# Interleaving the bidirectional scans of a Mamba-2 block with the next group's projections, and moving the decay behind the product of state and C

## The chip, the cores and the metric

The kernel runs on one core of a Trainium2 chip. The metric is device time in microseconds of one launch. The core's engines are TensorE (PE in the profile; PEld is its weight load), VectorE (DVE), ScalarE (ACT) and GpSimd (POOL); SyncE (SP) only issues transfers here. ScalarE and GpSimd issue transfers too.

## What is computed

One encoder block over 1040 tokens (16 learned ones and 1024 of the input), width 1024, all in float32:

```python
u = rms_norm(h, w_norm_mix)
proj = u @ w_in                     # 9344 columns: conf_a, conf_g, z, xbc, dt, gates
c = depthwise_conv31(conf_a * sigmoid(conf_g)); c = silu(layer_norm(c))
xbc = silu(depthwise_conv7(xbc))    # xs: 32 heads x 64; B, C: 4 groups x 128
# each direction d, in chunks of 128 tokens; a_cs is the cumulated dt*A inside a chunk, xd = x*dt
y_diag = (C B^T * exp(a_cs[l] - a_cs[s]) masked) @ xd
states = B^T @ (exp(a_cs[-1] - a_cs) * xd)
S = S * exp(a_cs[-1]) + states                 # from chunk to chunk
y_off = exp(a_cs) * (C @ S_before)
y = y_f + y_b + D * xs
y = rms_norm(y * silu(z)); merged = gates * (c @ w_conf_out), gates * (y @ w_ssm_out)
h = h + merged @ w_out
out = rms_norm(h + expert_choice_ffn(rms_norm(h)))   # 16 experts, 130 tokens each
```

## The kernel before

Everything is kept transposed, channels on the 128 partitions and the 1040 tokens along the free axis. A planner orders the instructions of each engine: it goes through the program in the order written, simulates, and issues what is ready by priority; `tc.high_priority(offset=n)` moves what is inside ahead by n. Each engine, and each queue of transfers, then runs its list strictly in order.

**Projections.** w_in is taken in 73 tiles of 128 columns. `Columns` loads the raw tiles on SP's queue (L191) in groups of four, takes a norm for a scale (L192 to L206), and splits each tile into a high and a low half-precision part (L217, L218), one tile ahead. `proj` multiplies in three pieces of some 346 tokens ("thirds" below), each 24 matmuls (L96 to L98) into one of three PSUM buffers (mm).

**Stage b1** holds dt, four conf tiles, all 24 xbc tiles, eight gate tiles and four z tiles. An xbc tile is convolved with 7 taps on VectorE (L436), passes a Silu (L437), and goes to memory channel-major (xbc_d) and, turned on TensorE, token-major (xk_d). A conf tile has 31 taps (L329) that are spread over what follows by `some_taps`.

**Scans.** For each of four groups of eight heads, `group` walks nine chunks in both directions: 18 calls of `half`. A half loads the row of cumulated decays of its eight heads, copied to all partitions (L512), and the token-major x and B (L506, L510). ScalarE forms E = exp(-relu(cs - row)) (L524, L525) and overwrites the row with exp(row) (L527); VectorE multiplies E by the masked product of B and C (L543) and row by C (L528). TensorE adds both terms in py (L550): xw times E, and the state S times row. VectorE adds py to xs, in the first of the two directions together with the D skip (L558, L555). The new state is made from st_ps (L565, L570, L571); GpSimd makes xw (L516). The unmasked direction's product of B and C goes through memory (cb_d) to the half that needs it later.

The scans have a priority of 3000. Behind every pair of halves one of the remaining projections is written (`filler`): four conf, twelve z and eight gate tiles over the four groups. After the groups come the output products of the SSM branch, whose weights `split_w` splits into buffers of the pool wsp (L158, L159), allocated behind the scans, then the norm of the conf branch, the merge, and 16 experts.

Of the kernel before, what the change touches and what calls it, by code (L numbers as in the profile page):

```python
# [13 lines left out]
OP = mybir.AluOpType  # L14
# [31 lines left out]
def tile_block(ctx, tc, x, meta_tokens, w_norm_mix, w_in, w_conf_dw, b_conf_dw, conf_ln_g, conf_ln_b,  # L46
# [10 lines left out]
    xbc_d = dram.tile([24, P, T], F32, name="xbc_d")  # L57
# [4 lines left out]
    xk_d = dram.tile([NTT, P, 20 * P], F32, name="xk_d")  # L62
    cs_d = dram.tile([64, T], F32, name="cs_d")
    cb_d = dram.tile([GR, NTT, P, P], F32, name="cb_d")
# [71 lines left out]
    wraw = wstack.enter_context(tpool("wraw", bufs=3))  # L136
    mps_stack = ctx.enter_context(ExitStack())
# [24 lines left out]
    with tpool("upool", side="right") as upool, tpool("stage", bufs=2, side="right") as stage, \  # L162
            tpool("bc") as bc, tpool("cfp") as cfp, ExitStack() as ostack:
# [10 lines left out]
        class Columns:  # L174

            def __init__(self, order):
                self.order, self.raw, self.split, self.at, self.groups = order, {}, {}, 0, 0

            def group(self):
                b = 4 * self.groups
                cols = self.order[b:b + 4]
# [4 lines left out]
                sq = w16.tile([P, 4], F32, name="sq")  # L188
                for i, col in enumerate(cols):
                    t = r16.tile([P, KD, P], F32, name="wr16")  # L190
                    nc.sync.dma_start(t, w_in[0][:, col:col + P].rearrange("(k p) c -> p k c", p=P))  # L191
                    act.activation(out=junk, in_=t, func=AF.Square, accum_out=sq[:, i:i + 1])  # L192
                    self.raw[b + i] = t
                sqb = w16.tile([P, 4], BF, name="sqb")
                dve.tensor_copy(sqb[:, :n], sq[:, :n])
                ps = mps.tile([P, 512], F32, name="mm")
                pe.matmul(ps[:, :n], onesb, sqb[:, :n], start=True, stop=True)
                sc = w16.tile([P, 4, 4], F32, name="sc", bufs=3)
                sci = sc.bitcast(I32)
                dve.tensor_scalar_max(sc[:, 0, :n], ps[:, :n], 1e-36)  # L200
                dve.tensor_scalar(sci[:, 0, :n], sci[:, 0, :n], 24, 23, op0=OP.logical_shift_right,
                                  op1=OP.logical_shift_left)
                dve.tensor_scalar(sci[:, 1, :n], sci[:, 0, :n], -1.0, float(204 << 23), op0=OP.mult, op1=OP.add)
                dve.tensor_scalar(sci[:, 2, :n], sci[:, 0, :n], float(50 << 23), None, op0=OP.add)
                dve.tensor_scalar_mul(sc[:, 2, :n], sc[:, 2, :n], su[:, 1:2])
                dve.tensor_scalar_mul(sc[:, 3, :n], sc[:, 2, :n], 0.5)  # L206
# [3 lines left out]
            def convert(self, n):  # L210
# [3 lines left out]
                wh = w16.tile([P, KD, P], F16, name="wh", bufs=3)  # L214
                wl = w16.tile([P, KD, P], F16, name="wl", bufs=3)
                with tc.high_priority(offset=400):
# [4 lines left out]
            def take(self, col):  # L221
# [4 lines left out]
                if n == 0:  # L226
                    self.group()
                    self.convert(0)
                if n % 4 == 0:
                    self.group()  # L230
# [4 lines left out]
        order = [OFF_DT]  # L235
        for i in range(4):
            order += [i * P, D + i * P]
            for m, j in enumerate((4 * i, 4 * i + 1, 4 * i + 2, 4 * i + 3, 16 + i, 20 + i)):
                order.append(OFF_XBC + j * P)
                if m in (2, 5):  # L240
                    order.append(OFF_GATE + (2 * i + (m == 5)) * P)
            order.append(OFF_Z + i * P)
        for g in range(GR):
            order += [(4 + g) * P, D + (4 + g) * P]
            order += [OFF_Z + j * P for j in range(4 + 4 * g, min(8 + 4 * g, 16))]
            order += [OFF_GATE + j * P for j in range(8 + 2 * g, 10 + 2 * g)]
# [1026 lines left out]
```

## Time and profile before

| | us |
|---|---|
| three runs | 3096.0, 3101.21, 3108.91 (median 3101.21) |
| the profiled execution, its own time | 3112.4 |
| its span in the trace | 3110.7 |
| first norm and setup | 0 to 60 |
| projections of stage b1 | 60 to 560 |
| scans with the other projections | 560 to 1262 |
| output products, merge, w_out, routing | 1262 to 1760 |
| experts and final norm | 1760 to 3110 |

Over the span TensorE is busy 90%, VectorE 72%, ScalarE 54%, GpSimd 24%. In the profile's rows, "x" is a count of instructions, "busy" the time in which at least one of a group runs (matmuls are pipelined and overlap, so the mean of one can exceed busy over count), and "idle before" the engine's idle time ahead of them with what ended it. The granted clock is the share of TensorE's full speed that it got.

### The profile page before, as it was taken

What the parts mean: (1) busy time and instruction counts of PE and PEld (TensorE: products, weight loads), DVE (VectorE), ACT (ScalarE), POOL (GpSimd) and SP (SyncE); (2) the same over time, 40 slices, a digit from 0 to 9 for tenths busy, and PEclk for the clock granted to TensorE, in tenths of its full rate; (3) what the DMA queues carried; (4) which work ended last, traced back from release to release, by engine and by line L of the source; (5) the groups of instructions that cost most, each with busy time, mean ns of one, the idle gap of its engine ahead of it and who ended that gap; (6) DMA issues with size and microseconds to landing.
All of it is one profiled execution on the core that took longest, in us unless ns stands there. A gap on an engine that the chain in (4) does not pass through costs nothing. (4 is left out here: it accounts for less than half of the span.)

```text
span 3110.7 us, 65955 instructions
## 1 busy us (share of the span) xinstructions
PE 2787.0 (90%) x28098; PEld 2372.4 (76%) x28098; DVE 2231.9 (72%) x2849; ACT 1684.7 (54%) x2502; POOL 735.0 (24%) x677
## 2 busy tenths in 40 slices
PE   5999999887878788399999798999999999999996
PEld 4666666554545455388987698999999999999996
DVE  5969779486877795867745587767777766677773
ACT  6545445554746464243413376666666666666653
POOL 1101011344544643312000001212222222221213
PEclk9999999997988898699999899999999999999998
DMA  5334233776777665421533598999999999999994
GB/s 158 93 110 137 90 117 126 176 145 190 146 207 159 169 120 140 144 93 52 161 118 121 208 325 300 334 325 338 327 334 320 319 321 333 335 328 334 335 332 148
DMA packets 425975, 666.03 MB, mean 214 GB/s; under 512 B 29217, under 2 KB 213953, under 8 KB 425673
## 3 DMA queue, kind: packets, MB, share of 16 engines
q1 hardware_dynamic: 366032, 514.83, 52.3%
q0 software_dynamic: 25760, 73.27, 7.9%
q10 hardware_dynamic: 33888, 73.71, 7.5%
q8 instruction: 220, 3.60, 0.5%
q14 instruction: 75, 0.61, 0.1%
HBM read 585.15 MB, written 76.59 MB: 213 GB/s over the span
## 5 line engine op out<-in xcount | busy, mean ns | idle before, releaser
L96 PE MATMUL gu<-xT,wh 128*128 128x130 f16 x3968 | 701.5, 223 | 3.0 <-ACT sil L1046 2.7
L97 PE MATMUL gu<-xT,wh 128*128 128x130 f16 x3968 | 701.2, 220 | 0.0
L98 PE MATMUL gu<-xT,wl 128*128 128x130 f16 x3968 | 700.3, 221 | 0.9 <-DVE wl L1017 0.9
L1003 ACT ACTIVATE junk<-wst 128x2048 bf16<-128x2048 f32 x248 | 473.7, 1910 | 389.4 <-DMA wst<-in_w_exp_gate_dram 329.6
L97 PEld LDWEIGHTS <-wh 128*128 128x128 f16 x5720 | 568.8, 99 | 108.5 <-issue 21.2
L96 PEld LDWEIGHTS <-wh 128*128 128x128 f16 x5720 | 562.7, 98 | 113.8 <-issue 17.0
L98 PEld LDWEIGHTS <-wl 128*128 128x128 f16 x5720 | 560.7, 98 | 102.2 <-issue 13.9
L1017 DVE SCALAR_TENSOR_TENSOR wl<-wst,sc,wh 128x2048 f16<-128x2048 f32 x248 | 572.8, 2346 | 26.9 <-ACT wh L1014 23.0
L96 PE MATMUL mm<-uh,wh 128*128 128x346 f16 (+2 forms) x1752 | 557.5, 318 | 1.5 <-ACT pre L432 0.9
L97 PE MATMUL mm<-ul,wh 128*128 128x346 f16 (+2 forms) x1752 | 557.0, 318 | 0.0
L98 PE MATMUL mm<-uh,wl 128*128 128x346 f16 (+2 forms) x1752 | 556.9, 318 | 0.0
L1069 PE MATMUL dn<-ac,wst 128*128 128x130 f32 x3840 | 459.4, 277 | 0.0
L1069 PEld LDWEIGHTS dn<-ac,wst 128*128 128x128 f32 x3840 | 440.7, 191 | 0.0
L1088 POOL DMA_INDIRECT h<-yo,idx x60 | 184.2, 3070 | 918.9 <-DVE yo L1087 764.4
L329 DVE SCALAR_TENSOR_TENSOR co<-ci,ct,co 128x1040 f32<-128x1040 f32 x240 | 344.6, 1436 | 3.3 <-ACT co L326 1.3
L524 ACT ACTIVATE E<-row,cst 128x128 f32<-128x128 f32 (+1 forms) x576 | 170.3, 377 | 204.9 <-DMA row<-cs_d 189.4
L1014 ACT ACTIVATE wh<-wst,sc 128x2048 f16<-128x2048 f32 x124 | 241.3, 1995 | 17.5 <-DVE sc L980 16.5
L516 POOL TENSOR_TENSOR xw<-xk,dtw 128x512 f32<-128x512 f32 (+1 forms) x136 | 200.2, 1475 | 208.4 <-PE py L550 74.8
L96 PE MATMUL mm<-yh,wh 128*128 128x346 f32 (+1 forms) x480 | 159.5, 332 | 63.4 <-ACT wh L158 48.5
L550 PE MATMUL py<-E,xw 128*64 128x128 f32 (+1 forms) x1152 | 126.7, 301 | 85.4 <-DVE E L543 46.2
L436 DVE SCALAR_TENSOR_TENSOR po<-pre,sp,po 128x1040 f32<-128x1040 f32 x144 | 184.8, 1294 | 2.6 <-ACT po L434 1.8
L543 DVE TENSOR_TENSOR E<-E,cbm 128x1024 f32<-128x1024 f32 (+1 forms) x72 | 97.6, 1355 | 94.9 <-ACT E L525 94.2
(347 smaller groups left out, 4285.8 us busy)
## 6 DMA issues: line engine op xcount, KB each, us to landing
wst<-in_w_exp_gate_dram SPq DMA_DIRECT2D x128, 1024.0 KB, 8.3
wst<-in_w_exp_up_dram SPq DMA_DIRECT2D x128, 1024.0 KB, 8.2
wst<-in_w_exp_down_dram SPq DMA_DIRECT2D x128, 1024.0 KB, 9.8
wr<-in_w_in_dram SPq DMA_DIRECT2D x73, 512.0 KB, 4.2
row<-cs_d SPq DMA_DIRECT2D x64, 512.0 KB, 10.4
xk<-xk_d ACTq DMA_DIRECT2D x64, 256.0 KB, 5.9
xbc_d<-po POOLq DMA_DIRECT2D x24, 520.0 KB, 3.2
xk_d<-xt POOLq DMA_DIRECT2D x20, 512.0 KB, 4.0
```

The source lines that it names most:

```text
L96: pe.matmul(ps, wh(k), xh(k), start=(k == 0), stop=False)
L97: pe.matmul(ps, wh(k), xl(k), start=False, stop=False)
L98: pe.matmul(ps, wl(k), xh(k), start=False, stop=(k == K - 1))
L329: dve.scalar_tensor_tensor(co, ci[:, m:m + T], ct[:, m:m + 1], co, op0=OP.mult, op1=OP.add)
L436: dve.scalar_tensor_tensor(po, pre[:, m:m + T], sp[:, j, m:m + 1], po, op0=OP.mult, op1=OP.add)
L516: pool.tensor_mul(heads(o[:L]), heads(xk[:L]), dtw[:L, c, w, hs].unsqueeze(2).to_broadcast([L, HG, 64]))
L524: act.activation(out=E[:L, j, :L], in_=row[:L, j, :L], func=AF.Relu, scale=-1.0, bias=cs)
L1003: act.activation(out=junk, in_=t[m][b], func=AF.Square, accum_out=sq[:, b, m:m + 1])
L1014: act.activation(out=wh[m][0], in_=t[m][0], func=AF.Copy, scale=sc[:, 1, m:m + 1])
L1017: dve.scalar_tensor_tensor(wl[m][b], t[m][b], sc[:, 1, m:m + 1], wh[m][b], op0=OP.mult, op1=OP.subtract)
L1069: pe.matmul(last["dn"][b // 3][:, b % 3], t[:, k, b * P:b * P + P], ac[:, 2 * i + k], start=(i + k == 0 and b % 3 == 0), stop=(i == 7 and ...
L1088: nc.gpsimd.indirect_dma_start(out=h2_d[b], in_=yo[:, h], in_offset=None, compute_op=OP.add, out_offset=bass.IndirectOffsetOnAxis(ap=r.idx ...
```

## The change

- The xbc tiles of groups 1 to 3, the other conf, z and gate tiles are cut into thirds (generators) and spread evenly over the 18 halves of the group before: 42, 48, 45 and 48 thirds in the four groups. Only dt, the xbc tiles of group 0, one conf, two gates and one z tile come before the first scan.
- Both directions' E of a chunk are one unit (`within`), written two halves ahead of their use at a priority of 600; E is made in the row's own buffer, and both products of B and C are masked at once, so cb_d is gone. `add_within` adds both directions into one py.
- The decay no longer multiplies C. `pass_state` multiplies S by C on TensorE into yo, VectorE multiplies yo by er = exp(a_cs), which is made once in `do_dt` and loaded from ecs_d, and GpSimd adds it to xs. The D skip is a copy of xs by ScalarE at the start of a group.
- Memory is laid out by group (xs_d, bc_d, xk_d) and by chunk (cs_d, ecs_d). All loads of the scans are on SP's queue. The raw tiles have six buffers (wraw, wraw2) in groups of three; the split tiles use wsp, which is now allocated at the start.

```diff
-    xbc_d = dram.tile([24, P, T], F32, name="xbc_d")
+    xs_d = [dram.tile([4, P, T], F32, name=f"xs_d{g}") for g in range(GR)]
+    bc_d = [dram.tile([2, P, T], F32, name=f"bc_d{g}") for g in range(GR)]
...
-    cs_d = dram.tile([64, T], F32, name="cs_d")
-    cb_d = dram.tile([GR, NTT, P, P], F32, name="cb_d")
+    cs_d = dram.tile([NTT, 64, P], F32, name="cs_d")
+    ecs_d = dram.tile([NTT, 2, 32, P], F32, name="ecs_d")
...
+    wsp = wstack.enter_context(tpool("wsp", bufs=2))
...
-                    t = r16.tile([P, KD, P], F32, name="wr16")
+                    t = (wraw if (b + i) % 6 < 3 else wraw2).tile([P, KD, P], F32, name="wr")
...
+        first = [("xbc", 0, 4), ("conf", 0), ("xbc", 0, 5), ("xbc", 0, 0), ("gate", 0), ("xbc", 0, 1), ("xbc", 0, 2),
+                 ("xbc", 0, 3), ("gate", 1), ("z", 0)]
...
+        plan = [mixed([1], xbc[1], zt[1:4] + gt[0:3]), mixed([2, 3], xbc[2], zt[4:8] + gt[3:5]),
+                mixed([4], xbc[3], zt[8:12] + gt[5:8]), mixed([5, 6, 7], [], zt[12:16] + gt[8:14])]
...
+                    def fill(upto):
+                        while done[0] < int(upto):
+                            next(work, None)
+                            done[0] += 1
...
+                    def within(c):
...
+                        for d in range(2):
+                            row = s2.tile([P, HG, P], F32, name="row", bufs=4)
+                            nc.sync.dma_start(row[:, :, :L], cs_d[c, 32 * d + h0:32 * d + h0 + HG, :L].partition_broadcast(P))
+                            rows.append(row)
+                        xk = load_xk(c)
...
+                        for d, E in enumerate(rows):
...
+                                act.activation(out=E[:L, j, :L], in_=E[:L, j, :L], func=AF.Relu, scale=-1.0, bias=cs)
+                            act.activation(out=E[:L, :, :L], in_=E[:L, :, :L], func=AF.Exp, scale=-1.0)
+                            xw = scaled(xk, c, 0, d)
+                            dve.tensor_mul(E[:L, :, :L], E[:L, :, :L],
+                                           cbm[d][:L, :L].unsqueeze(1).to_broadcast([L, HG, L]))
+                            terms.append((xw, E))
...
+                    def state(d, c):
...
+                            xk = load_xk(c)
+                            xw = scaled(xk, c, 1, d)
+                        if c != (8 if d else 0):
+                            er = s2.tile([P, 4, P], F32, name="er")
+                            q = 4 * (4 * d + g)
+                            for hh in range(2):
+                                nc.sync.dma_start(er[64 * hh:64 * hh + 64, :, :L],
+                                                  ecs_d[c, hh, q:q + 4, :L].partition_broadcast(64))
...
+                    def pass_state(d, c, S, ops):
...
+                            yo = sps.tile([P, 4, P], F32, name="yo", bufs=2)
+                            for i in range(4):
+                                pe.matmul(yo[:, i, :L], S[:, P * i:P * i + P], Ct[:, t0:t0 + L], start=True, stop=True)
+                            with tc.high_priority(offset=700):
+                                dve.tensor_mul(er[:, :, :L], yo[:, :, :L], er[:, :, :L])
+                                xx = xs[:, :, t0:t0 + L]
+                                pool.tensor_add(xx, xx, er[:, :, :L])
...
+                    with ahead():
+                        units = [within(0)]
+                        ops = [state(*halves[0]), state(*halves[1])]
+                        nc.sync.dma_start(xs, xs_d[g].rearrange("i p t -> p i t"))
+                        for i in range(4):
+                            act.activation(out=xs[:, i], in_=xs[:, i], func=AF.Copy, scale=d2[:, 4 * g + i:4 * g + i + 1])
+                    fill(4)
+                    for n, (d, c) in enumerate(halves):
+                        with ahead():
+                            if n % 2 == 0 and n // 2 + 1 < NTT:
+                                units.append(within(n // 2 + 1))
+                            if n + 2 < len(halves):
+                                ops.append(state(*halves[n + 2]))
+                        if n % 2 == 0:
+                            add_within(n // 2, units.pop(0))
+                        fill(4 + (total - 4) * (n + 0.5) / len(halves))
+                        S[d] = pass_state(d, c, S[d], ops.pop(0))
+                        fill(4 + (total - 4) * (n + 1) / len(halves))
+                        some_taps(4 if g in (1, 3) else 2)
...
-                        with tc.high_priority(offset=3000):
-                            S[d] = half(d, 8 - i if d else i, S[d])
-                        some_taps(3)
-                    filler(g)
...
-    wsp = wstack.enter_context(tpool("wsp", bufs=2))
```

## Rows read from the trace of the kernel before

**Rows 1.** Busy time by stretch: engines, then TensorE's granted clock, transfer share, GB/s.

```profile
60.00:560.00 500.00, 497.95 (x3434) 337.24 (x3433) 413.80 (x436) 246.67 (x385) 61.25 (x141) 1.00 0.35 110
560.00:1262.00 702.00, 565.46 (x4376) 370.18 (x4374) 528.50 (x683) 378.86 (x857) 321.56 (x277) 0.88 0.69 160
1262.00:1309.00 47.00, 0.42 (x1) 0.43 (x2) 36.04 (x23) 15.52 (x16) 19.23 (x8) 0.53 0.37 106
```

**Rows 2.** Waits of three engines, 560 to 1262 us: total, times, longest.

```profile
ACT E L524 <- DMA row<-cs_d: 189.4, 48, 16.3
...
DVE E L543 <- ACT E L525: 94.2, 19, 17.1
...
PE py L550 <- DVE E L543: 46.2, 13, 12.3
```

**Rows 3.** Busy time in two windows of 40 us, columns as in rows 1.

```profile
560.00:600.00 40.00, 28.74 (x170) 17.37 (x169) 10.27 (x21) 25.71 (x64) 13.10 (x11) 0.83 0.90 228
...
640.00:680.00 40.00, 35.16 (x314) 24.21 (x314) 39.96 (x58) 21.21 (x46) 22.61 (x19) 1.00 0.76 159
```

**Rows 4.** Costliest groups of the whole span: shapes, count, busy us, mean ns.

```profile
L96 PE MATMUL mm<-uh,wh 128*128 128x346 f16 (+2 forms) x1752 | 557.5, 318 | 1.5 <-ACT pre L432 0.9
...
L1069 PE MATMUL dn<-ac,wst 128*128 128x130 f32 x3840 | 459.4, 277 | 0.0
```

**Rows 5.** A wait of TensorE, and the timeline of GpSimd, 1200 to 1340 us.

```profile
PE mm L96 <- ACT wh L158: 47.1, 1, 47.1
...
1302.31 0.57 POOL L332 DMA_DIRECT2D conf_d<-co  x1
```

**Rows 6.** Timeline of TensorE inside one half, start and length in us.

```profile
1200.62 0.41 PE L550 MATMUL py<-row,S 128*64 128x128 f32 x4
1200.84 0.41 PE L550 MATMUL py<-E,xw 128*64 128x128 f32 x4
```

**Rows 7.** Groups of instructions of VectorE by shape, 560 to 1262 us.

```profile
L329 DVE SCALAR_TENSOR_TENSOR co<-ci,ct,co 128x1040 f32<-128x1040 f32 x105 | 161.5, 1539 | 2.0 <-ACT co L326 1.3
L543 DVE TENSOR_TENSOR E<-E,cbm 128x1024 f32<-128x1024 f32 x64 | 93.8, 1466 | 52.2 <-ACT E L525 51.4 <-DMA cbm<-cb_d 0.5
L528 DVE TENSOR_TENSOR row<-row,Ct 128x1024 f32<-128x1024 f32 x60 | 83.4, 1391 | 5.3 <-ACT row L527 5.3
...
L558 DVE SCALAR_TENSOR_TENSOR xs<-xs,d,py 128x128 f32<-128x128 f32 x128 | 35.9, 335 | 1.5 <-PE py L550 1.5
...
L555 DVE TENSOR_TENSOR xs<-xs,py 128x512 f32<-128x512 f32 x32 | 21.3, 674 | 13.1 <-PE py L550 13.0
```

**Rows 8.** The same of ScalarE, 560 to 1262 us.

```profile
L524 ACT ACTIVATE E<-row,cst 128x128 f32<-128x128 f32 x512 | 157.5, 388 | 167.4 <-DMA row<-cs_d 159.1 <-DVE S L571 5.1 <-POOL xw L516 1.8
L525 ACT ACTIVATE E<-E 128x1024 f32<-128x1024 f32 x64 | 66.9, 1045 | 6.2 <-PE st_ps L565 5.3 <-ACT E L524 0.3 <-ACT row L527 0.2
L527 ACT ACTIVATE row<-row 128x1024 f32<-128x1024 f32 x60 | 62.5, 1041 | 0.0
```

**Rows 9.** Instructions of two lines: ns min/median/max, first and last start in us.

```profile
L437 ACT ACT_TABLE_LOAD  x1: 1283/1283/1283, 118.9 to 118.9; - x1
...
L525 ACT ACT_TABLE_LOAD  x1: 1283/1283/1283, 581.2 to 581.2; - x1
```

**Rows 10.** Groups of GpSimd by shape, 560 to 1262 us.

```profile
L516 POOL TENSOR_TENSOR xw<-xk,dtw 128x512 f32<-128x512 f32 x124 | 183.0, 1479 | 179.7 <-PE py L550 73.4 <-DMA xk<-xk_d 45.6 <-PE st_ps L565 45.2
L570 POOL TENSOR_TENSOR S<-S,etot 128x512 f32<-128x512 f32 x56 | 80.1, 1430 | 13.7 <-DVE S L571 10.7 <-ACT S L568 3.0
```

**Rows 11.** The conv tap on VectorE in stage b1, 56 to 560 us.

```profile
L329 DVE SCALAR_TENSOR_TENSOR co<-ci,ct,co 128x1040 f32<-128x1040 f32 x120 | 155.3, 1294 | 0.9
```

**Rows 12.** Issues of transfers: KB each, median us to landing; 560 to 1262, then 60 to 560 us.

```profile
row<-cs_d SPq DMA_DIRECT2D x64, 512.0 KB, 10.4
...
wr<-in_w_in_dram SPq DMA_DIRECT2D x45, 512.0 KB, 4.0
```

**Rows 13.** A wait of SP's queue, 60 to 560 us: total, times, longest.

```profile
SPq L191 <- DVE wl L218: 426.9, 38, 22.5
```

More of the change, by code (lines that the diff above doesn't have):

```diff
@@ L174, in tile_block, with __init__, group @@
         class Columns:
[L178 to L183, printed above, removed]
+            G = 3
+            def __init__(self):
+                self.order, self.raw, self.split, self.at, self.groups = [], {}, {}, 0, 0
+            def group(self, behind=None):
+                b = self.G * self.groups
+                cols = self.order[b:b + self.G]
                 self.groups += 1
@@ L342, in gate_tile @@
                 ps = proj(w, t0, n)
-                act.activation(out=st[:, t0:t0 + n], in_=ps, func=AF.Tanh, scale=w[3])
+                with soon():
+                    act.activation(out=st[:, t0:t0 + n], in_=ps, func=AF.Tanh, scale=w[3])
+                yield
             nc.gpsimd.dma_start(gate_d[j], st)
@@ L434, in do_xbc @@
-                act.activation(out=po, in_=pre[:, 0:T], func=AF.Identity, scale=sp[:, j, 0:1], bias=sp[:, j, 7:8])
+                yield
+            po = b1.tile([P, T], F32, name="po", bufs=2)
+            act.activation(out=po, in_=pre[:, 0:T], func=AF.Identity, scale=sp[:, j, 0:1], bias=sp[:, j, 7:8])
+            with tc.high_priority(offset=200):
                 for m in range(1, TS):
@@ new lines, in tile_block, with turn @@
+        later, third = [], [0]
+        def turn(g, i, po, xt, c0):
+            cs = range(c0, min(c0 + 4, NTT)) if c0 else range(1)
+            ps = mps.tile([P, 512], F32, name="mm").rearrange("p (c q) -> p c q", q=P)
+            for c in cs:
+                t0, L = TOK[c]
+                pe.transpose(ps[:L, c - c0], po[:, t0:t0 + L], ident)
+            L = TOK[c0][1]
+            with soon():
+                act.activation(out=xt[:L, c0:c0 + len(cs)], in_=ps[:L, :len(cs)], func=AF.Copy)
+            cols = slice(i * P, i * P + P)
+            if c0 == 0:
+                nc.gpsimd.dma_start(xk_d[g][0, :NMETA, cols], xt[:NMETA, 0])
+            elif c0 == 5:
+                nc.gpsimd.dma_start(xk_d[g][1:, :, cols].rearrange("c p n -> p c n"), xt[:, 1:])
@@ new lines, in thirds @@
+        def thirds(items):
+            for kind, *a in items:
+                for _ in makers[kind](*a):
+                    third[0] += 1
+                    if later and later[0][0] <= third[0]:
+                        later.pop(0)[1]()
+                    yield
+        with tpool("b1") as b1:
+            with tpool("dts") as b0, tpool("dtps", bufs=2, space=PSUM) as b0ps:
+                dt = do_dt(b0, b0ps)
+                next(dt)
+                work = thirds(first)
+                for n, _ in enumerate(work):
+                    if n == 10:
+                        next(dt, None)
+                    if n > 5:
+                        some_taps(2)
+                while later:
+                    later.pop(0)[1]()
+            with tpool("s1", bufs=1) as s1, tpool("s2", bufs=2) as s2, \
+                    tpool("sps", bufs=1, space=PSUM) as sps:
@@ L596, in ones_sum @@
+                for g in range(GR):
+                    group(g)
     def ones_sum(src, fin):
```

456 lines of the change are left out of this document (216 added, 240 removed).

## The prediction

> **What bounds the kernel now.** I read the stretches first [rows 1]. From 60 to 560 us there are projections alone: TensorE is busy 497.95 of 500 us at a granted clock of 1.00 (its 2.4 GHz level), so it is the bound. From 560 to 1262 us the scans of the four groups run between the other projections, and TensorE is busy 565.46 of 702 us at a mean clock of 0.88, between its two levels. That is 565.46 x 0.88 = 498 us of full-speed work, so 204 us are lost. VectorE is busy 75% of that stretch, ScalarE 54%, GpSimd 46%: no engine is full, so the stretch waits on latency. The waits say where [rows 2]: ScalarE waits 189.4 us in 48 places for the row of decays (L524), VectorE 94.2 us for ScalarE's Exp, TensorE 46.2 us for VectorE's product. It is one chain, load to ScalarE to VectorE to TensorE, walked 72 times (4 groups, 18 halves). Forty-microsecond windows show both ends [rows 3]: the start of group 0 gives TensorE 28.74 us at clock 0.83, and a covered window gives 35.16 us at clock 1.00, with VectorE full (39.96 us). So VectorE is next in line where the chain is hidden.
>
> How much there is to hide it with: a projection matmul takes 497.95 / 3434 = 0.145 us; 73 column tiles share 3 x 1752 of them [rows 4], 72 each, so a tile costs 10.4 us and a third of a tile 3.5 us. The stretch of the scans holds 28 tiles (292 us), and 498 - 292 = 206 us are matmuls of the scans.
>
> One hole lies behind it: from 1262 to 1309 us TensorE does 0.42 us of work [rows 1]. It waits 47.1 us for ScalarE's first split weight (L158). That comes only after the last conv result has been stored (conf_d, issued at 1302.31 us) [rows 5].
>
> **The change part by part.** *TensorE.* Its projections, transposes, E products and state products stay. The term of state and C goes from 1024 matmuls with 64 columns of weights to 512 with 128. The old ones start four in 0.22 us [rows 6], 55 us in all. The nearest row for the new ones is the expert's down projection, fp32 128x128 on 130 columns: 459.4 / 3840 = 0.12 us [rows 4], 61 us in all. So +6 us: 498 + 498 + 6 = 1002 us of full-speed work after 60 us.
>
> *VectorE.* Gone are the product of row and Ct (83.4 us) and the fused add with the D skip (35.9 us). New are 64 products of yo and er, at the price of the add from PSUM of the same form, 0.674 us: 43 us [rows 7]. The other adds into xs stay 36, the masked cb products 72. Net -76 us.
>
> *ScalarE.* The second Exp over the row goes, 62.5 us; 16 copies of xs by the D skip come, at 1.045 us each (the Exp of 1024 columns), 17 us [rows 8]. One wait is added in kind: Silu of the next group now stands among Exps. Before, one table load stands at the first Silu (118.9 us) and the next at the first Exp of the scans (581.2 us), none at a Tanh between [rows 9]. So the two functions need different tables. Groups 0 to 2 each take in 6 Silus, every one between two E blocks: 18 x 2 = 36 loads x 1.283 us = 46 us. ScalarE's sum stays as it was (-62 + 17 + 46), at 626 us of some 1100, and its idle time hides them; without that cover they cost 46 us. The Trainium skill, "ScalarE: Activation LUTs", What ACT_TABLE_LOAD costs, counts a drain of 1.38 us with each load, and its Table sets section asks for calls batched by set; by that the 36 would be 96 us, an estimate, and no row here shows the drain.
>
> *GpSimd.* 64 adds of er into xs, at 1.43 to 1.48 us (its other products of that size): 93 us [rows 10]; the 32 cb stores go. It stays under half busy. But what it reads costs VectorE: the conv tap takes 1.294 us where GpSimd rests [rows 11] and 1.539 us in the scans, while the add from PSUM keeps 0.674 us [rows 7]. That is 16% of the tap's time; 16% of the taps, the E and the row products there (161.5 + 93.8 + 83.4 us) is 54 us, beside 263 us of GpSimd products [rows 10], so 93 us more bring about 19. The Trainium skill, "SBUF — State Buffer", Who interferes with whom, says that a VectorE instruction with two SBUF inputs contends with a GpSimd one that reads SBUF; the two rows agree.
>
> VectorE then: 413.80 + 528.50 - 76 + 19 = 885 us, and the taps now left behind 1262 us (within 36.04 us of work there [rows 1]): some 915 us in about 1100. It is close, not the bound. Groups 1 and 3 carry two and three convs, so there it is near full.
>
> *Loads.* The row load stays 512 KB, but one run of 4 KB for a partition instead of eight of 512 B. It took 10.4 us to land [rows 12]; I take 6, between nothing gained and the 4 us in which a 512 KB weight landed in the projections [rows 12]. Moved from ScalarE's queue to SP's are xk, Bt, Ct, xs and sz; 128 er loads are new, cb's store and reload go. On SP all of these now stand in line with weight loads, and those waited there 426.9 us in 38 places for a converted tile [rows 13], harmless while nothing else was queued. Six raw buffers replace eight, in groups of three: some six more small scale chains, about 1 us each, hidden by the raw tiles ahead.
>
> *The lost 206 us* (2 before 560, 204 after). 61 tiles, 183 thirds, now lie beside 72 halves: 2.5 thirds, 8.8 us, a half, where 28 tiles gave 4 us. A half lasts about 12.3 us, so the lead of two slots is about 25 us. What has to fit is the load (10.4 us at worst), two blocks of E on ScalarE (2 x 4.1 us) and two products of 1.47 us: 22 us. It fits, narrowly. Bounds: nothing lost (as from 60 to 560 us, with VectorE at 83%), or 206 us again (a half loses as much as now). Nearer to which? The four group starts lose 6 to 20 us each in windows like the first of [rows 3], some 55 us, and keep half: the next group's xs can only be loaded when the last group's sum is out. The other 150 us are 2 us a half. The longer lead and the thicker filler hide most of it, but evacuations share three PSUM buffers with the transposes, and ScalarE's E blocks of 8 us stand in front of them: I leave 1 us a half. 27 + 70 = 97; I take 95 us.
>
> *The hole at 1262 us.* The weights' buffers (wsp) no longer wait for the end of the conv pool, and the last conv, stored 40 us after the last projection, now gets its input 12 thirds before it. What is late next is y itself: its load lands, and ScalarE and VectorE split four tiles. I leave 22 of 47 us; bounds 10 and 47.
>
> **Sum.** The projections and scans end at 60 + 1002 + 95 = 1157 us instead of 1262: -105 us. The hole gives -25 us. 3112.4 (the profiled execution) - 130 = 2982 us. That execution stands 11 us above the median of the runs, so the forecast is 2971 us in their terms. What follows 1309 us isn't touched.
>
> **The rivals**, in median terms.
> 1. *The loss stays.* TensorE's queue holds projections in order, so a half that is late stops them too; if every half loses 2 us and every group its start as now, the end is 1062 + 206 = 1268 us, and only the hole gains: 3101 + 6 - 25 = 3082 us. For it: VectorE near full in groups 1 and 3, one py buffer. Against: 76 us taken from VectorE and the chain begun two slots earlier.
> 2. *The loss nearly goes.* Projections as filler keep TensorE at clock 1.00, as from 60 to 560 us, where VectorE was busy at 83% as it will be. With 30 us lost and a hole of 10 us: 3101 - 170 - 37 = 2894 us.
> 3. *The table loads land on the path*: each delays an E block that TensorE is waiting for, 46 us on top of the forecast: 3017 us. For it: Exp to VectorE to TensorE is the chain of [rows 2]. Against: the lead. The Trainium skill's rule of batching by set ("ScalarE: Activation LUTs", Table sets) speaks for it.
> 4. *Slower: rows and er stuck behind weight loads on SP.* The 61 weight loads of the groups wait as before, 11.2 us each (426.9 / 38), 683 us in all, and the loads of the scans stand behind them. TensorE feels only what exceeds the lead. From 225 us lost in all (33%) nothing is gained; at half, 340 us lost in place of 95, with the hole's gain: 1062 + 340 = 1402, so 3101 + 140 - 25 = 3216 us. Against: where a load waits for a tile, TensorE is working on tiles already there, and the order may put the scans' loads first.
>
> **How the numbers follow.** Forecast 0.45, rival 1 0.13, rival 2 0.22, rival 3 0.10, rival 4 0.10. A measurement of this kernel can tell about 0.5% (15 us) from no change. Rival 1 at 3082 us is only 19 us faster, so half of it counts as no change, and a little of the forecast's tail does: faster 0.83, same 0.08, slower 0.09. The range leaves out the slower rival, the slow half of rival 1 and the fast edge of rival 2: 2888 to 3080 us. The forecast's own range is 2930 to 3015 us.
>
> **What would show it.** Right: projections and scans end near 1157 us with TensorE's mean clock from 180 us on at 0.95 or more; ScalarE's wait for the row load falls from 189.4 us to under 60; VectorE's products with Ct are gone and the yo products take about 0.68 us; some 36 table loads of 1.283 us, before Exps and Silus alone; the wait for L158's split under 25 us. Wrong: a wait of ScalarE for row or of GpSimd for xk that stays over 150 us (rival 4, if SP's own waits for wl stand before them); VectorE over 95% busy between 300 and 1150 us (rival 1); GpSimd tap prices above 1.6 us, which would make VectorE the bound; transposes or py that hold TensorE for xs at each group's start.

## The result, and the profile after

The changed kernel takes 3073.45 us (median of 4 runs, 3070.57 to 3077.56) against 3100.83 us (3096.0 to 3108.91): a ratio of 0.991, 95% interval 0.9885 to 0.9935. It is 27 us faster where 130 us were forecast: inside the range, with the right sign, next to the first rival (3082 us).

Busy time by stretch, after, columns as in [rows 1]; the last projection ends at 1243 us:

```profile
60.00:560.00 500.00, 435.56 (x3003) 292.23 (x3001) 376.53 (x413) 288.02 (x566) 179.22 (x187) 0.94 0.49 155
560.00:1243.00 683.00, 610.64 (x4269) 414.13 (x4270) 563.49 (x611) 337.88 (x675) 292.10 (x264) 0.95 0.51 161
1243.00:1275.00 32.00, 3.07 (x12) 2.73 (x10) 17.75 (x15) 3.42 (x5) 4.20 (x7) 0.57 0.88 308
```

Busy time times granted clock gives 409 and 580 us of full-speed work: 989 us, as forecast (1002). Lost are 91 us before 560 us and 103 behind it; before, it was 2 and 204 [rows 1]. The loss hardly shrank; nearly half of it now lies in a stretch that had lost nothing. The projections end 19 us earlier instead of 105.

Waits of all engines, after, 60 to 1243 us (total, times, longest):

```profile
ACT junk L197 <- DMA wr<-in_w_in_dram: 169.8, 40, 12.2
ACT row L581 <- DMA row<-cs_d: 106.0, 28, 15.2
POOL pre L367 <- DVE po L378: 92.2, 13, 41.5
POOL xs L630 <- DVE er L628: 85.0, 24, 12.9
POOL xw L556 <- DMA xk<-xk_d: 82.6, 23, 10.1
POOL sz_d L360 <- DVE st L358: 79.2, 11, 23.9
...
PE mm L392 <- ACT po L379: 34.5, 8, 12.5
...
PE mm L97 <- DVE st L358: 19.1, 12, 3.3
...
PE st L570 <- DVE S L641: 15.6, 8, 4.1
```

ScalarE's longest wait in total is for raw weight tiles; the one for rows is down from 189.4 us [rows 2], though not under the 60 us that the prediction named. New ones stand on GpSimd: it waits to clear a buffer's edge until VectorE has finished its taps, up to 41.5 us at a time, with the scans' products, states and additions in its queue behind. TensorE's largest wait is new as well: a transposition of an xbc tile that waits for the Silu behind the 7-tap conv.

Groups by shape, 60 to 1243 us, VectorE, GpSimd and ScalarE (three views), answering to [rows 7 to 11]:

```profile
L335 DVE SCALAR_TENSOR_TENSOR co<-ci,ct,co 128x1040 f32<-128x1040 f32 x237 | 352.1, 1486 | 3.8 <-ACT co L332 1.7
...
L584 DVE TENSOR_TENSOR row<-row,cbm 128x1024 f32<-128x1024 f32 x64 | 106.8, 1696 | 4.7 <-ACT row L582 4.7
...
L628 DVE TENSOR_TENSOR er<-yo,er 128x512 f32<-128x512 f32 x60 | 40.8, 680 | 9.2 <-PE yo L626 4.9 <-DMA er<-ecs_d 2.3 <-issue 2.0
```

```profile
L556 POOL TENSOR_TENSOR xw<-xk,dtw 128x512 f32<-128x512 f32 x124 | 188.4, 1530 | 108.7 <-DMA xk<-xk_d 61.5 <-PE st L633 30.9 <-PE py L596 8.6
L630 POOL TENSOR_TENSOR xs<-xs,er 128x512 f32<-128x512 f32 x60 | 97.6, 1628 | 76.2 <-DVE er L628 76.0
```

```profile
L379 ACT ACT_TABLE_LOAD x19 | 24.4, 1283 | 0.3
...
L582 ACT ACT_TABLE_LOAD x18 | 23.1, 1283 | 0.3
```

Issues of transfers (median us to landing, last column), answering to [rows 12], and TensorE's wait in the hole, answering to [rows 5]:

```profile
row<-cs_d SPq DMA_DIRECT2D x64, 512.0 KB, 5.0
```

```profile
PE mm L97 <- ACT yh L750: 31.0, 2, 28.9
```

Where TensorE's idle time lies, by how busy VectorE was in the same window of 20 us (windows, idle us; counted from the view by stretch):

| VectorE busy | before, 60 to 1260 | after, 60 to 1240 | before + layout, 60 to 1180 |
|---|---|---|---|
| 19 us or more | 24, 26.7 | 27, 66.0 | 34, 46.2 |
| 14 to 19 us | 15, 42.7 | 16, 40.6 | 9, 14.3 |
| under 14 us | 21, 68.7 | 16, 30.2 | 13, 27.2 |

Before, half of TensorE's idle time lay in windows where VectorE was idle for much of the time too. With the layout alone this part falls from 68.7 to 27.2 us, so much of it was waiting for loads. After, half of the idle time lies in windows that VectorE fills.

### The profile page after: what moved, and what is told of

The parts are those of the page before. It is cut to its first block, busy times and chain, and to the rows that moved or that the text cites. A ratio compares the mean times of both kernels' runs of the same rounds, so it can differ in the third digit from the quotient of the medians.

```text
span 3075.9 us, 64985 instructions
## 1 busy us (share of the span) xinstructions
PE 2772.1 (90%) x27584; PEld 2372.7 (77%) x27584; DVE 2214.2 (72%) x2747; ACT 1683.7 (55%) x2499; POOL 827.2 (27%) x714
## 3 DMA queue, kind: packets, MB, share of 16 engines
q1 hardware_dynamic: 335376, 580.64, 55.4%
## 5 line engine op out<-in xcount | busy, mean ns | idle before, releaser
L98 PEld LDWEIGHTS <-wh 128*128 128x128 f16 x4856 | 480.9, 99 | 82.8 <-issue 38.2
L97 PEld LDWEIGHTS <-wh 128*128 128x128 f16 x4856 | 475.3, 98 | 51.7 <-issue 7.6
L99 PEld LDWEIGHTS <-wl 128*128 128x128 f16 x4832 | 471.3, 98 | 47.5 <-DVE wl L1105 1.5
L335 DVE SCALAR_TENSOR_TENSOR co<-ci,ct,co 128x1040 f32<-128x1040 f32 x240 | 356.0, 1484 | 3.8 <-ACT co L332 1.7
L97 PE MATMUL mm<-uh,wh 128*128 128x346 f16 (+3 forms) x888 | 280.6, 316 | 22.7 <-DVE st L358 11.2
L97 PE MATMUL mm<-uh,wl 128*128 128x346 f16 (+1 forms) x864 | 275.9, 319 | 17.6 <-DVE st L358 7.9
L98 PE MATMUL mm<-ul,wh 128*128 128x346 f16 (+3 forms) x888 | 280.2, 316 | 0.0
L99 PE MATMUL mm<-uh,wh 128*128 128x346 f16 (+3 forms) x888 | 279.3, 315 | 0.0
L98 PE MATMUL mm<-ul,wl 128*128 128x346 f16 (+1 forms) x864 | 275.3, 319 | 0.0
L99 PE MATMUL mm<-uh,wl 128*128 128x346 f16 (+1 forms) x864 | 275.3, 319 | 0.0
L556 POOL TENSOR_TENSOR xw<-xk,dtw 128x512 f32<-128x512 f32 (+1 forms) x136 | 200.5, 1486 | 129.9 <-DMA xk<-xk_d 82.6
L581 ACT ACTIVATE row<-row,cst 128x128 f32<-128x128 f32 (+1 forms) x576 | 168.9, 378 | 108.0 <-DMA row<-cs_d 106.0
L378 DVE SCALAR_TENSOR_TENSOR po<-pre,sp,po 128x1040 f32<-128x1040 f32 x144 | 204.4, 1420 | 2.7 <-ACT po L375 1.6
```

What stands on the lines that cost most here:

```text
L97: pe.matmul(ps, wh(k), xh(k), start=(k == 0), stop=False)
L98: pe.matmul(ps, wh(k), xl(k), start=False, stop=False)
L99: pe.matmul(ps, wl(k), xh(k), start=False, stop=(k == K - 1))
L335: dve.scalar_tensor_tensor(co, ci[:, m:m + T], ct[:, m:m + 1], co, op0=OP.mult, op1=OP.add)
L378: dve.scalar_tensor_tensor(po, pre[:, m:m + T], sp[:, j, m:m + 1], po, op0=OP.mult, op1=OP.add)
L556: pool.tensor_mul(heads(o[:L]), heads(xk[:L, :512]), dtw[:L, c, w, hs].unsqueeze(2).to_broadcast([L, HG, 64]))
```

## The experiments

Kernels were compared on several chips, so the last column puts each ratio on one scale: (ratio - 1) x 3101 us. Each ratio is uncertain by 0.2 to 0.5%, some 6 to 16 us.

| run | ratio to before, 95% | us against before |
|---|---|---|
| the change | 0.991 [0.9885, 0.9935] | -28 |
| before_layout | 0.9787 [0.9744, 0.9829] | -66 |
| after_old_rows | 1.0201 [1.0166, 1.0235] | +62 |
| before_decay | 0.9937 [0.9913, 0.9961] | -20 |
| layout_dec | 0.9858 [0.9831, 0.9886] | -44 |
| layout_dec_dve | 0.9795 [0.9763, 0.9826] | -64 |
| half_taps (of the change) | 0.975 [0.9701, 0.98] | -78 |
| before_half_taps | 0.979 [0.9758, 0.9821] | -65 |
| no_pool_add | 0.9731 [0.9674, 0.9787] | -83 |
| dve_add | 0.9861 [0.9818, 0.9904] | -43 |
| er4 | 0.9906 [0.9869, 0.9942] | -29 |
| conf_last | 0.9924 [0.99, 0.9948] | -24 |
| no_silu | 0.9871 [0.9821, 0.9921] | -40 |
| pool_free | 0.9846 [0.9812, 0.988] | -48 |
| pool_free_dve | 0.9853 [0.9818, 0.9889] | -46 |
| pool_free_tanh | 0.9814 [0.9798, 0.9831] | -58 |
| layout_g3 | 0.966 [0.9628, 0.9693] | -105 |
| layout_dec_dve_g3 | 0.9725 [0.9691, 0.9758] | -85 |
| layout_c6 | 0.975 [0.973, 0.977] | -78 |

**First look: four suspects in the changed kernel.** One deeper buffer, and three pieces of work left out.

```
half_taps:    taps.extend([... for m in range(1, TK, 2)])       # was range(1, TK)
er4:          er = s2.tile([P, 4, P], F32, name="er", bufs=4)   # was 2
no_silu:      act.activation(out=po, in_=po, func=AF.Tanh)      # was Silu
no_pool_add:  - pool.tensor_add(xx, xx, er[:, :, :L])
```

> The changed kernel with every second tap of the 31-tap conv left out (15 of 30 for each conv tile, so the conv branch is not the reference's). Theory V: VectorE is the bound in the middle of the groups (full 20 us windows are where TensorE falls to 12 to 17 of 20), so 120 taps of 1.49 us less (178 us) give TensorE back half or more of its lost time: 60 to 120 us, some 2960 to 3010 us. Rivals Q (er loads hold up SP's queue), T (table loads on the path) and J (chain latency at the group joins): none of these hangs on the taps, 0 to 15 us.

> The changed kernel with four buffers for er instead of two. Theory Q: SP's queue stands 232 us in 51 places before an er load until GpSimd has added the old er, and weight loads stand behind it (ScalarE waits 170 us for weights): freeing them gives 20 us or more, 3050 us or less. Theory V: the weights are not what TensorE waits for; within 8 us of the changed kernel's 3073 us, SP's wait before er falls to under 80 us.

> The changed kernel with Tanh in place of Silu behind the 7-tap conv (other values, same length), so that no table load stands between Exp and Silu: 37 loads of 1.283 us go. Theory T: they delay E blocks that TensorE waits for, the time falls by 25 to 46 us, to 3030 to 3048 us. Theory V: ScalarE's idle time hides them, within 8 us of 3073 us.

> The changed kernel without GpSimd's 64 adds of er into xs (the state's term is left out of y): 98 us less of GpSimd reading SBUF. Theory V: VectorE's instructions with two SBUF inputs get shorter (E product from 1.70 to some 1.5 us, taps from 1.49 to some 1.42 us), some 30 us of VectorE, and the time falls by 15 to 35 us, to 3040 to 3058 us. Theory T or J: under 8 us. Theory Q would also gain here, and er4 tells it apart.

Against the changed kernel, half the taps are worth 50 us and GpSimd's addition 55 us: less and more than theory V expected. The exchange of tables (12 us) and the deeper buffer (1 us) lie inside the uncertainty. Work on VectorE, or beside it, counts.

About theory Q er4 says nothing, because the wait that it was to take away stayed. SP's wait before an er load, 60 to 1243 us, in the changed kernel and then in er4:

```profile
SPq L613 <- POOL xs L630: 232.4, 51, 11.2
```

```profile
SPq L613 <- POOL xs L630: 228.8, 50, 11.8
```

So loads that hold each other up on SP's queue stay open as one cause, and some of no_pool_add's 55 us may be theirs: SP's wait before er fell to 161.8 us there. TensorE's own waits in the changed kernel have none for a converted weight tile and 5.1 us around a tile's scale. An indirect cost is possible, since ScalarE waits 169.8 us for raw tiles with Silus and E blocks in its queue behind. Before, it waited 91.3 us for them from 60 to 560 us, and TensorE lost only 2 us there.

**Where the taps lie, and who adds.** In conf_last the conv tiles stand at the end of the opening and of each group's projections; in dve_add VectorE adds.

```
conf_last:  items.insert((i + (1 if xs_ else 0)) * len(items) // len(confs), ("conf", j))
dve_add:    dve.tensor_add(xx, xx, er[:, :, :L])                # was pool
```

> The changed kernel with the conv tiles moved: the first one last before the scans, and those of groups 0 to 2 last in their third or half of the group, so that their taps are there at the start of the next group, where VectorE idles (3 to 8 of 20 us at 200, 460 and 1000 us) while it is full in the middle. The work is the same. Theory V2 (VectorE's work lies unevenly: idle at the group joins, full behind them): the time falls by 20 to 50 us, to 3025 to 3055 us, and the turns' wait for the 7-tap conv (34.5 us) falls. Theory J (joins wait on the chain of loads and turns whatever VectorE does): within 8 us of 3073 us.

> The changed kernel with VectorE adding er into xs instead of GpSimd: +43 us of VectorE at 0.67 us an add, -98 us of GpSimd reading. Leaving the add out gave 62 us. If that was VectorE slowed by GpSimd's reads (theory C, about 30 us of VectorE by the durations), the exchange is about even: 3060 to 3085 us. If it was GpSimd's lateness (er and xw late behind the adds, theory G), most of the 62 us comes: 3020 to 3045 us.

The place of the conv tiles did not matter (4 us slower, inside the uncertainty). VectorE's addition gains 15 us, which fits neither theory well. It cost VectorE more than expected, 0.924 us each (55.4 us in all), while 240 taps fell from 1.486 to 1.403 us and 64 products from 1.696 to 1.383 us, some 40 us together.

**The change's parts on the kernel before.** The layout by chunk alone, the decay part alone, and the layout undone in the changed kernel (code shortened).

```
before_layout:   cs_d = dram.tile([NTT, 64, P], F32, name="cs_d")
                 nc.gpsimd.dma_start(cs_d[0, :, :NMETA], v[:, :NMETA])
                 nc.gpsimd.dma_start(cs_d[1:].rearrange("c h l -> h c l"), ...)
                 nc.sync.dma_start(row[:, :, :L], cs_d[c, hs, :L].partition_broadcast(P))
before_decay:    - exp(row); row *= Ct; py += S, row
                 + yo = S, Ct; er = yo * er; pool.tensor_add(xx, xx, er)   # row bufs 3, py bufs 1
after_old_rows:  cs_d = dram.tile([64, T], ...)                            # the changed kernel
                 nc.sync.dma_start(row[:, :, :L], cs_d[..., t0:t0 + L].partition_broadcast(P))
```

> The kernel before with one part of the change: the decays laid out by chunk, so that a row load reads one run of 4 KB for a partition instead of eight of 512 B. If the load's 10.4 us is what the chain of the scans waits for (189.4 us of ScalarE), it lands in some 5 us and the time falls by 20 to 60 us, to 3040 to 3080 us; if it is the chain behind the load, under 10 us.

> The kernel before with one part of the change: the decay applied to the product of state and C (Exp and product over row gone, yo, er and GpSimd's add come, three row buffers instead of four, one py buffer). By the forecast's own terms VectorE loses 84 us and gains 43 us and the adds stay, so if VectorE's work counts as it stands: 10 to 40 us faster. If GpSimd's add costs as in the changed kernel (62 us): same or slower, 3095 to 3130 us.

> The changed kernel with one part undone: the cumulative sums stay in one table of 64 rows of the sequence, so that a row load again fetches eight runs of 512 bytes for each partition. The same layout alone, given to the kernel before, was worth 67 us. Theory R (the layout is worth as much here, and the rest of the change gives back some 45 us): 3115 to 3145 us, row loads back at about 10 us, and ScalarE's wait for them well above its 106 us. Theory H (issued a whole chunk ahead, the loads are hidden either way, so that the layout is worth little in the changed structure): 3070 to 3090 us, with the loads at 10 us all the same.

The layout alone gains 66 us, more than twice the whole change. The decay alone gains 20 us. Before_layout's issues, its waits from 560 to 1180 us and its stretches:

```profile
row<-cs_d SPq DMA_DIRECT2D x64, 512.0 KB, 5.1
xk<-xk_d ACTq DMA_DIRECT2D x64, 256.0 KB, 3.7
```

```profile
ACT E L525 <- DMA row<-cs_d: 78.9, 24, 17.0
```

```profile
60.00:560.00 500.00, 497.58 (x3425) 336.87 (x3424) 413.98 (x436) 246.13 (x384) 61.93 (x142) 1.00 0.35 110
560.00:1178.00 618.00, 534.55 (x4383) 352.55 (x4380) 532.85 (x682) 376.91 (x857) 346.47 (x277) 0.94 0.56 182
1178.00:1228.00 50.00, 3.00 (x12) 2.82 (x11) 39.82 (x26) 18.06 (x18) 20.03 (x9) 0.53 0.38 116
```

The row lands in half the time, and other traffic lands sooner too (xk 3.7 us instead of 5.9); the wait falls from 189.4 to 78.9 us, and the loss in the scans from 204 to 618 - 534.55 x 0.94 = 116 us, with the opening still at 1.00. The hole behind it stays. The Trainium skill, "DMA: Bandwidth & Descriptors", Specifications, gives 512 B as the least transfer for line rate. By that the eight runs of 512 B cost nothing; the trace doesn't agree: 10.4 us against 5.1 for the same 512 KB.

Undone in the changed kernel it costs 90 us (1.0201 against 0.991). There the row took 11.1 us, and two queues felt it, ScalarE's and, behind the rows on SP, that of GpSimd's operand (60 to 1320 us):

```profile
ACT row L580 <- DMA row<-cs_d: 187.0, 55, 15.8
POOL xw L555 <- DMA xk<-xk_d: 183.3, 31, 11.9
```

So theory R holds, and the 3155 us even lie above its range: the longer lead does not hide the loads. Without the layout the rest of the change makes the kernel 62 us slower.

**Layout and decay together, in the old order**, with GpSimd's and with VectorE's addition.

```
layout_dec:      before_layout + before_decay, pool.tensor_add(xx, xx, er[:, :, :L])
layout_dec_dve:  the same,                     dve.tensor_add(xx, xx, er[:, :, :L])
```

> The kernel before with two parts of the change, the layout by chunk (alone 67 us) and the decay on the product of state and C with GpSimd's addition (alone 17 us), and without the new order of the stage. If the two gains add: 3010 to 3020 us. If both remove the same lateness (the wait for rows that only the decay's second use of them made long), 3025 to 3035 us. If the decay, with VectorE free of the loads' waits, is now paid for by GpSimd's addition and the slower VectorE beside it: 3035 to 3060 us.

> As the run before, but VectorE adds the product into xs in place of GpSimd. In the changed kernel this move was worth 15 us (between the two theories of that run). Theory G (GpSimd's reads and lateness cost more than VectorE's own 41 us of additions): 10 to 25 us below the run before. Theory V (VectorE is what ends the stage, so its own additions count in full): 10 to 30 us above the run before.

The gains don't add: on top of the layout the decay costs 22 us with GpSimd's addition and nothing (2 us) with VectorE's. The two runs differ in that addition alone, so they price GpSimd's reads. VectorE's groups, 60 to 1243 us, first layout_dec, then layout_dec_dve:

```profile
L330 DVE SCALAR_TENSOR_TENSOR co<-ci,ct,co 128x1040 f32<-128x1040 f32 x240 | 364.0, 1517 | 1.1
...
L552 DVE TENSOR_TENSOR E<-E,cbm 128x1024 f32<-128x1024 f32 x64 | 116.0, 1813 | 0.4 <-ACT E L532 0.3
...
L586 DVE TENSOR_TENSOR S<-st_ps,S 128x512 f32<-128x512 f32 x56 | 38.0, 679 | 2.7 <-PE st_ps L580 1.6 <-POOL S L585 1.0
```

```profile
L330 DVE SCALAR_TENSOR_TENSOR co<-ci,ct,co 128x1040 f32<-128x1040 f32 x240 | 335.5, 1398 | 1.1
...
L552 DVE TENSOR_TENSOR E<-E,cbm 128x1024 f32<-128x1024 f32 x64 | 93.4, 1463 | 0.0
...
L575 DVE TENSOR_TENSOR xs<-xs,er 128x512 f32<-128x512 f32 x60 | 57.9, 966 | 0.6
```

60 additions of GpSimd (95 us there) lengthen taps and E by 364.0 + 116.0 - 335.5 - 93.4 = 51 us, about what VectorE takes to add itself (57.9 us); the sum from PSUM (S, 679 ns) is untouched. The Trainium skill, "SBUF — State Buffer", Who interferes with whom, lets a VectorE instruction with two SBUF inputs contend with a GpSimd one that reads SBUF, and leaves one with a single SBUF input free outside the two-port modes; both agree.

**A control: half the taps in the kernel before.** The edit is that of half_taps.

> Control on the kernel before: every second of the 30 depthwise taps of the eight conv tiles is left out, as in the run on the changed kernel, where it was worth 49 us. Theory E (in the kernel before VectorE waits for the row loads rather than the stage for VectorE; only in the changed kernel did VectorE become what ends the stage): the projections end within 15 us of 1262, the kernel gains 0 to 25 us, and what it gains lies behind 1262, where the last taps are. Theory B (VectorE's work bounds both kernels alike): the projections end 40 us or more earlier and the kernel gains 45 to 70 us.

Theory E falls: the kernel before gains 65 us, and in the trace the projections end near 1204 us instead of 1262. VectorE's queue was part of the chain there too, at 75% busy. Not all of the gain lies there: the wait for the split weight in the hole falls from 47.1 us [rows 5] to 10.0. The two traced executions are 99 us apart, so these differences are larger than those of the medians.

**GpSimd's queue in the changed kernel** (code shortened; the first two lines are pool_free).

```
- pool.memset(ci / pre edges, 0.0)         + dve.memset(...)
- nc.gpsimd.dma_start(gate_d / xs_d / bc_d / xk_d, ...)   + nc.scalar.dma_start(...)
pool_free_dve:   and dve.tensor_add(xx, xx, er[:, :, :L])
pool_free_tanh:  pool_free, and AF.Tanh for AF.Silu
```

> The changed kernel, with what GpSimd does for the projections taken off its queue: the edges of the conv buffers are cleared by VectorE, and the stores of gates, xbc tiles and turned tiles are issued by ScalarE, which makes their data. In the changed kernel GpSimd waited 92 us in 13 times with a clearing for VectorE's taps, and some 150 us with stores for ScalarE or VectorE, with the scans' products, additions and states queued behind. Theory K (this queue is where the new order gives its gain back): 3020 to 3055 us, 20 us or more below the 3073 of the changed kernel. Theory W (the waiting costs nothing, since the scans' work is far enough ahead, and VectorE's work or the length of the scans' chain sets the time): 3065 to 3085 us.

> As the run before, and VectorE adds the product into xs in place of GpSimd (alone worth 15 us on the changed kernel). If GpSimd's lateness was the addition's trouble, freeing the queue leaves little for this move: within 8 us of the run before. If it is GpSimd's reads beside VectorE (products of E at 1.70 us, taps at 1.49 us), which the freed queue doesn't lessen: 12 to 20 us below the run before.

> The changed kernel with GpSimd's queue freed of the projections' clearings and stores (alone 0.9846) and with Tanh, which the same table holds as Exp, in place of Silu in the xbc tiles, so that the stage exchanges no tables (alone 0.9871, against 0.991 for the changed kernel). If the two costs add: 0.979 to 0.982, some 15 us under pool_free. If both only let the same late work through sooner: 0.983 to 0.987.

Freeing the queue gains 20 us: theory K. GpSimd's wait in pool_free, 60 to 1243 us:

```profile
POOL xs L630 <- DVE er L628: 173.5, 30, 18.1
```

It now waits twice as long (85.0 us before this edit) for the product that it adds: it is there ahead of it, no longer late. TensorE's wait for the Silu falls with it, from 34.5 to 20.7 us. And VectorE's addition brings nothing more. Without the exchange of tables another 10 us come, as expected if the two costs add. The intervals overlap, so that this step is not sure by itself, but no_silu alone (12 us) agrees. By the Trainium skill, "ScalarE: Activation LUTs", What ACT_TABLE_LOAD costs, the 37 loads with their drains would be 98 us of ScalarE, an estimate. The trace shows loads of 1.283 us and, as for drains, nothing; some 10 to 12 us of their 47 came out as time.

**Another deal of the projections, in the old order.** Seven of the eight late gate tiles go to the fourth group (g3), or two conv tiles to the opening for four gate tiles (c6).

```
layout_g3:  fill.append([conf[g]] + zt[4 * g:4 * g + 4] + ([], [], gate[:1], gate[1:])[g])
layout_c6:  early, late = ((0,), (1,), (2, 4), (3, 5)), ((), (6,), (), (7,))
            late_g = (range(4, 7), range(7, 8), range(8, 11), range(11, 16))
```

> The kernel before with the layout by chunk (alone 67 us), and with seven of the eight late gate tiles of the scan stage projected in the fourth group and one in the third, in place of two in each. Theory U (the groups are limited by VectorE, and projections left over at a group's end run with VectorE half idle, so that dealing them to the last group, which has the fewest, evens the stage out): 10 to 30 us below the layout alone, 3000 to 3020 us. Theory W (the scans' chain sets each group's length, whatever is projected beside it, so that the deal doesn't matter): 3022 to 3038 us.

> Layout by chunk and decay on the product of state and C, added by VectorE, in the old order (3023 us, or 0.9795), with the same new deal of the gate tiles. In the run without it the last projection ended at 1080 us and the scans went on alone to 1200 us, with TensorE at some 12 of 20 us. Theory U: these 120 us take in six gate tiles (some 75 us of TensorE) that the first three groups no longer do, and the kernel gains 15 to 40 us, 2985 to 3010 us. Theory W: within 8 us of 3023.

> The kernel before with the layout by chunk (alone 0.9787) and another deal of the same projections: the conv tiles 4 and 5 with their taps move from the scan stage into the opening, where VectorE was busy 414 of 500 us, and four gate tiles, which need TensorE for as long but VectorE for nothing, move from the opening into the scan stage. Theory V (VectorE's work inside the scan stage sets its length): some 78 us of taps less in the stage end the projections 30 us or more before the 1177 us of the layout alone, and the kernel comes to 0.950 to 0.965 of the kernel before. Theory Z (as the run with the gates in the last group showed, only the taps that lie behind the last projection count): the projections end within 12 us of 1177, and the kernel comes to 0.964 to 0.972. If the opening can't take the taps: its projections end later than 560 us, and the kernel stays at 0.975 or above.

Layout_g3 is the best kernel of the study: 0.966, 77 us under the changed one. Its stretches (columns as in [rows 1]):

```profile
560.00:1180.00 620.00, 528.37 (x4368) 352.47 (x4366) 561.81 (x698) 380.54 (x859) 335.09 (x275) 0.95 0.57 184
...
1180.00:1228.00 48.00, 29.75 (x130) 27.32 (x131) 36.97 (x28) 22.32 (x31) 17.26 (x10) 0.75 0.47 158
```

But not for theory U's reason: the projections end at 1180 us, as with the layout alone, and the gain lies in the hole, where TensorE now works 29.75 of 48 us instead of 3.00 of 50. The last conv was stored at 1145.6 us instead of 1219.0, so the weights' buffers came free in time. With the decay as well (layout_dec_dve_g3) the deal gains 21 us, between its two theories, and that kernel stays 20 us behind layout_g3. In layout_c6 the stage of the scans shrank to 567 us (640 to 1207) from 618, as theory V wants for 78 us of taps less; but the opening grew by 80 us. There is one conv input buffer, and TensorE waits 21.8 us there for VectorE to finish with it, and 14.9 us for the Silu of an xbc tile. So the third case of its expectation came, and where VectorE's taps could go is not settled.

## Why the prediction was wrong

**The step that failed** is "The lost 206 us": 95 us were left of it, and it was 194, of which 137 are idle time of TensorE and the rest its clock. The step counted the chain of a half as bare durations (22 us) against a lead of 25 us, and concluded "It fits, narrowly"; evacuations and transposes got a part of "1 us a half". TensorE's waits, which add up to its idle time, show what came instead (all of its waits, by the instruction that waited; 60 to 1262 us before, 60 to 1243 after):

| us of TensorE's waits, ahead of | before | after |
|---|---|---|
| the scans' products and states | 135.6 | 47.3 |
| transposes of xbc tiles | 1.0 | 47.2 |
| projections, for a PSUM buffer to be emptied | 1.3 | 36.8 |
| a weight tile's scale | 0 | 5.1 |

So most of the chain was hidden, and the projections that were to hide it waited in its place. Their evacuations and Silus stand in the same queues as the scans' work: with E blocks on ScalarE, taps of 1.49 us on VectorE, stores and clearings on GpSimd. What each of these costs is shown only in part. That VectorE's queue counts is shown by two controls: half the taps gave 50 us after and 65 us before. But by the same sum as above (time less busy time at its clock, 60 us to the last projection) half_taps still loses some 147 of the 194 us, no_pool_add 157, pool_free 178: no run of the new order takes away more than a quarter, and what delays the rest stays open.

The first reading, "no engine is full, so the stretch waits on latency", was too simple: a mean of 75% was made of full windows and empty ones.

**The opening** had been the prediction's model of a stretch that loses nothing; 91 us were lost there. A third of them lies before the first product of the scans, which TensorE reaches at 233 us:

```profile
60.00:220.00 160.00, 136.12 (x876) 89.19 (x875) 119.58 (x140) 82.31 (x160) 17.51 (x40) 0.93 0.37 115
```

That is 33 us lost (160 - 136.12 x 0.93). Up to 230 us TensorE waits 18.8 us for the Silus of xbc tiles that it is to transpose; before, it waited 1.0 us for them in the whole stage.

**The layout** was sized rightly (6 us to land, 5.0 measured) and priced at nothing, as the lead was to cover even 10.4 us. It is worth 66 us in the old order and 90 us in the new. Taken as layout (-66), decay with GpSimd's addition (+22), all the rest, the new order above all (+16), the parts make up the -28 us of the change. Taken in another order they would share it otherwise, as the decay alone gained 20 us. The +16 is hardly more than its uncertainty, some 12 us; in it GpSimd's queue costs 20 us and the tables some 10 to 12, so that without them the rest gains some 15 us. Rival 3's 46 us for the tables came out as a quarter of that.

**Contention** was mis-sized: 19 us forecast, 51 us measured for the 95 us of additions in the old order, some 40 in the changed kernel. It ate what the decay took from VectorE (83.4 us of products gone, 40.8 us new), and the 7-tap conv, which now runs beside GpSimd's other products too, grew from 184.8 to 204.4 us of VectorE.

**The hole** was nearly right: 28.9 us of wait for y against 47.1, where 22 were forecast, and y is what is late next, as named.

**The rest held**: TensorE's work, yo products at 0.680 us (0.674), 37 table loads (36), additions of 97.6 us (93). TensorE's clock from 180 us on was 0.95, as named, and the loss stayed all the same, so that this sign told nothing. Rival 4, rows behind weight loads on SP, did not come in its size: ScalarE's wait for rows (106.0 us) and GpSimd's for xk (82.6 us) lie under the 150 us that it named. Whether it has a small share stays open, since er4 did not shorten the wait on SP. Rival 1 came in its size. Its sign, VectorE over 95% busy from 300 to 1150 us, did not: it was 80% (680.61 of 850 us). But in every group there are windows that VectorE fills; three of them and one of the slowest stretches, columns as in [rows 1]:

```profile
280.00:320.00 40.00, 32.51 (x227) 23.01 (x226) 40.00 (x36) 25.92 (x56) 29.05 (x22) 0.91 0.59 182
520.00:560.00 40.00, 33.50 (x223) 22.48 (x219) 40.00 (x42) 24.40 (x52) 24.52 (x20) 0.87 0.51 159
800.00:840.00 40.00, 34.24 (x257) 24.67 (x255) 40.00 (x39) 25.99 (x55) 29.22 (x23) 0.91 0.61 195
1060.00:1100.00 40.00, 26.96 (x172) 18.69 (x170) 39.79 (x36) 17.65 (x49) 25.16 (x17) 0.87 0.52 169
```

In the last of them no projection ran from 1076 us on, up to 1117: the order had put three chunks' scans in a row. What that bunching costs was not tried by itself, nor a second conv input buffer.

## What to carry to other kernels

When a change has a cheap part (here: store a table in the order in which it is read) and a large one, price and try the cheap part by itself; it held more than the whole gain. Count a chain that is to be hidden with the queues in which its instructions stand, GpSimd's stores and clearings too, and read how busy an engine is from windows of the length of one step, not from a mean. List all waits of the engine that bounds the stretch, before and after, and see that they add up to its idle time: here that showed the filler waiting where the chain had waited. When a buffer is made deeper, look whether the wait that it was to remove is gone. Look at what the last item in a stage leaves behind: which tile came last was worth 39 us.

## What was not expected of the hardware

The same 512 KB took 10.4 us as eight runs of 512 B for each partition and 5.1 us as one of 4 KB, and with the long run its neighbours landed sooner too (xk 3.7 us instead of 5.9). GpSimd's additions slowed a VectorE product of two SBUF operands from 1463 to 1813 ns and the tap from 1398 to 1517 ns, so that moving 58 us of VectorE's work to GpSimd saved VectorE 7 us.
